# A two-layer hybrid diffusion backbone on one core: products further from their sums, Fourier sums on VectorE, GLA state as 18 tiles, softmax sums spread by one transfer

## The chip, the cores and the metric

The kernel runs as one program on one core of a Trainium2 chip. The metric is the device time of one execution in microseconds (us). The kernel before took 2532.82 us, the median of three runs (2531.42 to 2536.8). Five engines work side by side, each through its own queue of instructions in order: TensorE (PE in the profile), VectorE (DVE), ScalarE (ACT), GpSimd (POOL), and SyncE (SP), which here issues the DMA transfers.

## The reference

```python
for l in range(2):                      # 2048 latent tokens, 256 context tokens, width 1024
    shift, scale, gate = split(silu_c @ w_ada[l] + b_ada[l], 3)       # for x and for ctx
    hx = rmsnorm(x, norm_w[l]) * (1 + scale_x) + shift_x              # hc likewise
    (f, fg, nq, nk, nv, ng, gq, gk, gv, gg, zf, zb) = split(h @ w_in[l])
    four = (fft2(f by 4 groups of 64).real) @ w_four[l]               # over positions x channels
    na   = softmax(8 x 16 window scores + bias, context scores) @ v   # 6 heads of 64
    gla  = gated linear attention in both directions, 4 heads, dk 48, dv 96, then RMSNorm
    mix  = concat(four * silu(fg), na * silu(ng), gla * silu(gg))
    x    = x + gate_x * (mix @ w_out[l])                              # ctx too in layer 0
return rmsnorm(x, norm_f)
```

## The kernel before

Each layer goes through stages, one after another: the input projections it needs first, the Fourier group (`four`, from about 155 us in layer 0 and 1430 us in layer 1), the neighbourhood attention (`na`, from 210 and 1525 us), the gated linear attention (`gla`, from 793 and 2004 us) and the output projection (from 1150 and 2350 us). Tokens are worked in blocks of 512 (0 to 3 latent, 4 the context, 256 wide). Weights are loaded in float32, scaled and split into a high and a low half of 16 bits, so one product is three matmuls for each of eight slices of the width.

**Order.** Instructions recorded through the class `Pin` keep the order of the program on their engine; all of them show as L72 in the profile. The others (in `four`, and the gate products of L313) are put in order by the build, which may bring a product forward.

**Fourier.** `four` takes three levels, `f1` to `f3`, each on half the length of the one before: VectorE forms the differences `od` of the two halves of `u` (L387), POOL their sums in place (L388), VectorE two copies of two elements (L390, L391) and four sums and differences into `fo` (L392 to L395); TensorE multiplies `fo` by the transform (L374), and what remains of `u` last. `four_g` makes the gates of one block: two halves `j`, each 24 matmuls 512 wide (L313); `gates()` asks for block 0 in layer 0, blocks 0 to 3 in layer 1, after the third level.

**Attention.** A unit is a pair `p` of heads and a block `b`; there are 15 in layer 0 and 12 in layer 1. A planner (`fill`) puts the unit's steps, the next unit's preparations and the side jobs (`side`) into one order, spread by position; a transfer counts as a step with a gap of 6 planner us behind it. Side jobs bring the weights of later stages in (`w_steps`): load (`a_`), four reductions `red` of `ws` into `wsm` on VectorE and their `rest`, a product of a diagonal `dg` (by ACT) with ones on TensorE that turns the column of scales into rows (`mm`), its inverse, and eight conversions to 16 bits in turn on ACT and VectorE. Other side jobs make `ada_row`, the modulation of the next layer, eight chunks of it with a transposition on TensorE (`s2`), and the scales of the output projection (`wo_scale`).

**Sums of the softmax.** The `tail` of each unit has the sums of two heads as rows of 512 in partitions 0 and 64 (`rs`). `out_` writes them to DRAM (`rsd`, L761), `in_` reads them back spread over the partitions, 4 or 8 numbers each (`rc`, L765), `rec` takes the reciprocal on VectorE and writes to DRAM (`rrd`, L769), `bc_` reads that back to all partitions (L773), and `fin` has POOL multiply gate `gt` and result `ob`.

**Last unit and GLA.** During the last unit, `gla_pre` loads `gva` and `gvb` (the weights of GLA's values) through the one staging buffer `ws`, sets up constants (`s0`, `s2`: `wst`, `wab`, `zt`) and does the first token tile's products (`half`). The tail of the last unit is finished inside `gla`: `na_tail(0)` is reciprocal and write, `na_tail(1)` the multiplications. `gla` works on 18 tiles of 128 tokens in the order 16, 17, 0 to 15: `decay`, `vproj`, `qz`, `kk` are products of TensorE, `cums` the cumulated decays, from which POOL makes `QK` (scaled queries and keys); `upd` writes the states into `SU`, and `chain` accumulates along it. `nst.close()` gives the attention's tiles free; behind it `ATm` (two of 128 x 1024) and `SU` (one tile of 128 x 18 x 384) are set up, both cleared by POOL.

Of the kernel before, what the change touches and what calls it, by code (L numbers as in the profile page):

```python
# [9 lines left out]
F32 = mybir.dt.float32  # L10
# [5 lines left out]
ALU = mybir.AluOpType  # L16
# [4 lines left out]
P = 128  # L21
DM = 1024
KB = 8
# [3 lines left out]
NT = T // P  # L27
# [50 lines left out]
def body(ctx: ExitStack, tc: tile.TileContext, a, out, dbg=None):  # L78
# [52 lines left out]
    def ada(l, pool):  # L131
# [4 lines left out]
        def chunk(c, pool=pool):  # L136
            v, te = Pin(tc, V), Pin(tc, TE)
            d = {}

            @dma_step  # L140
            def s0():
                d["w"] = pool.tile([P, KB * 256], F32, tag="ws", name="ws", bufs=1).rearrange("p (k n) -> p k n", k=KB)
                nc.sync.dma_start(out=d["w"], in_=a["w_ada"][l, c])
                d["row"] = pool.tile([P, 256], F32, tag="row", name="ada_row", bufs=1)[0:2, :]
                nc.sync.dma_start(out=d["row"], in_=a["b_ada"][l:l + 1, c * 256:(c + 1) * 256].to_broadcast([2, 256]))

            def s1():
# [12 lines left out]
            def s2():  # L160
                pt = bank("b")
                for q in range(2):
                    te.transpose(out=pt[:, 2 * q:2 * q + 2], in_=d["row"][:, q * P:(q + 1) * P], identity=ident[0:2, 0:2])
                v.tensor_copy(sc[:, :, 2 * c:2 * c + 2], pt[:, 0:4].rearrange("p (q w) -> p w q", w=2))

            return [s0, s1, s1b] + ([s2] if c < 8 else [])

# [77 lines left out]

    def load_a(l, name, fin=True, pin=False):
        off, n = GOFF[name]
        st = wp.tile([P, KB * 256], F32, tag="ws", name="ws", bufs=1)[:, 0:KB * n]
        d = nc.sync.dma_start(out=st, in_=a["w_in"][l, :, KB * off:KB * (off + n)])
        if pin:  # L250
            tc.keep_in_program_order(d)
        w = (l, n, st, wp.tile([P, 8], F32, tag="wsm", name="wsm", bufs=8))
        return sum_c(*sum_b(*sum_a(w))) if fin else w
# [72 lines left out]

    def four_g(ug, b, W, te=TE, s=S, v=V):
        t0, n = BLOCKS[b]
        for j in range(2):
            pt = bank("pj")  # L330
            proj_ch(pt, W, j * P, t0, n, te=te)
            x1 = ug["pool"].tile([P, 512], F32, tag="x1", name="x1", bufs=2)
            silu(x1[:, 0:n], ug["g"][:, j, t0:t0 + n], pt[:, 0:n], W, v, s)
# [5 lines left out]
    def four(l, last, ug, gates, hooks):  # L339
# [7 lines left out]
        with ExitStack() as st:  # L347
# [35 lines left out]
            for nm in ("f1", "f2", "f3"):  # L383
# [3 lines left out]
                V.tensor_tensor(out=od[:, :, 0:h], in0=lo_, in1=hi_, op=ALU.subtract)  # L387
                G.tensor_tensor(out=u[:, :, 0:h], in0=lo_, in1=hi_, op=ALU.add)  # L388
                q2 = q // 2
# [49 lines left out]
            hook(99)  # L439
            gates()  # L440
            for b in ([] if last else [4]) + [0, 1, 2, 3]:
# [23 lines left out]

    def w_steps(l, name, put=None, pool=None, part=None, d=None, pin=False, sc=True, tag="b"):
        d = {} if d is None else d
        v, s, te = Pin(tc, V), Pin(tc, S), Pin(tc, TE)

        @dma_step  # L470
        def a_():
            d["w"] = load_a(l, name, fin=False, pin=pin)

# [39 lines left out]
        if part == 1:  # L513
            return conv
        return [a_] + [lambda i=i: red(i) for i in range(4)] + [rest, mm, inv] + ([] if part == 0 else conv)

    def na(l, last, W, side, st):
        with ExitStack() as bst:
# [236 lines left out]
            def tail(p, b, d):  # L755
                n = BLOCKS[b][1]
                m = 2 * n // P

                def out_():
                    for h in range(2):  # L760
                        nc.sync.dma_start(out=rsd[0:1, h * n:(h + 1) * n], in_=d["rs"][h * 64:h * 64 + 1, 0:n])  # L761

                def in_():
                    d["rc"] = wk.tile([P, 8], F32, tag="rc", name="rc")
                    nc.sync.dma_start(out=d["rc"][:, 0:m], in_=rsd[0:1, 0:2 * n].rearrange("a (p e) -> (a p) e", e=m))  # L765

# [13 lines left out]

                return [out_, in_, rec, bc_, fin]

# [204 lines left out]
            SA = 0.1  # L987
            rsd, rrd = (dr.tile([1, 1024], F32, name=f"{z}{l}") for z in ("rsd", "rrd"))
            for h in range(2):
# [50 lines left out]
            last_ = tail(*units[-1], ds[-1])  # L1040
            run(last_[0:2])

            def fin_tail(v, g, k):
                if k:
                    last_[4](g)
                else:
                    last_[2](v)
                    last_[3]()

            return fin_tail  # L1050

    def gla_pre(l, st, wk, c, nxt):
# [59 lines left out]
        for i, z in enumerate(more):  # L1112
            steps.insert(QP + 2 * i, z)
        return steps
# [12 lines left out]
    def gla(l, last, W1, W2, pre, p2done, na_tail, nst):  # L1127
        order2 = list(range((NL if last else NT) - 1, -1, -1))
        with ExitStack() as st:
            with ExitStack() as st1_:  # L1130
# [19 lines left out]
                def chain(eng, act, c, n, p0, sa, sb_):  # L1150
                    pr = slice(p0, p0 + DK)
                    if act:
                        eng.tensor_tensor(out=DF[pr, c, :], in0=TOT[pr, :, sa, c], in1=TOT[pr, :, sb_, n], op=ALU.add)
                        act.activation(out=DF[pr, c, :], in_=DF[pr, c, :], func=AF.Exp, scale=1.0 / 16.0)
                    sv = SU[pr, n, :]
                    eng.tensor_tensor(out=sv, in0=sv, in1=SU[pr, c, :], op=ALU.add)
                    sv4 = sv.rearrange("p (h v) -> p h v", h=NH)
# [108 lines left out]
                def upd(it):  # L1266
# [5 lines left out]
                    if t in fnext:  # L1272
                        v.tensor_copy(SU[0:DK, fnext[t], :], pu[0:DK, 0:384])
                    if t in bnext:
                        v.tensor_copy(SU[64:112, bnext[t], :], pu[64:112, 0:384])

# [41 lines left out]
                gnw = kp0.tile([P, DV], F32, name="gnw")  # L1318
                nc.sync.dma_start(out=gnw, in_=a["gnw"][l:l + 1, :].to_broadcast([P, DV]))
                DF = kp0.tile([P, NT, NH], F32, name="DF")  # L1320
                for i in range(2):
                    ATm.append(kpb.tile([P, 2, 512], F32, name=f"ATm{i}"))
                    g.memset(ATm[i], 0.0)
                for t in (16, 17, 15, 0):
                    g.memset(SU[:, t, :], 0.0)
                for it in range(NT):
                    nx = it + 1 < NT
                    if 2 <= it < 16:
                        g.memset(SU[:, it - 1, :], 0.0)
                    if it > 0:  # L1330
# [9 lines left out]
                    if nx:  # L1340
                        kk(it + 1)
                        zT_(it + 1)
# [18 lines left out]
            with ExitStack() as st2_:  # L1361
# [44 lines left out]
                def inter(s_):  # L1406
                    s_["po"] = po = bank("a")
                    for h in range(NH):
                        te.matmul(out=po[:, h * DV:(h + 1) * DV], lhsT=s_["qt"][:, h * P:(h + 1) * P], rhs=SU[:, s_["t"], h * DV:(h + 1) * DV], start=True, stop=True)

# [66 lines left out]
    def wo_scale(l, c):  # L1477
# [24 lines left out]

        return [s0, s1] + ([lambda: None, s1b, s2] if c == 3 else [])

# [243 lines left out]
    for l in range(2):  # L1748
# [5 lines left out]

        def gates():
            for b in (0, 1, 2, 3) if last else (0,):
                four_g(ug[0], b, Wg)
# [21 lines left out]
        def side(p, b, wk):  # L1779
            n = p + 1  # L1780
            res = []
            if b == 0:
                res += w_steps(l, f"kv{n}", store(W, ("kv", n))) if n < 3 else w_steps(l, "gqz", store(nxt, "gqz"))
            if b == 2:
                res += w_steps(l, f"qg{n}", store(W, ("qg", n))) if n < 3 else w_steps(l, "gk", store(nxt, "gk"))
            if (p, b) == (2, 3):
# [199 lines left out]
```

## Time and profile before

| | |
|---|---|
| median of three runs | 2532.82 us (2531.42 to 2536.8) |
| the profiled execution | 2537.43 us, its span 2535.6 |
| TensorE busy | 2333.9 us, 92% |
| VectorE, ACT, POOL busy | 1609.2 (63%), 1126.5 (44%), 1117.4 (44%) |

The span is what the trace shows of the execution, from its first to its last instruction; the execution's own time is 1.8 us longer. TensorE runs at one of two clocks, and "granted clock" is the mean of a stretch as a share of the faster one. In a timeline, what stands in brackets is how long the engine had been idle before the instruction, and whose work ended that. "SPq" is a transfer being issued by SyncE.

### The profile page before, as it was taken

Reading aid. Unit: us, or ns where it says so; the run is one execution under the profiler, and the core shown is the slowest. Engines: PE = TensorE matmul, PEld = TensorE weight load, DVE = VectorE, ACT = ScalarE, POOL = GpSimd, SP = SyncE. Lnnn points to the kernel's source line nnn. Section 1 sums busy time; section 2 is a strip of 40 time slices with the busy share of each in tenths; the row PEclk is TensorE's granted clock in tenths of the full one; section 3 lists DMA queues with packets and bytes.
Section 4 is the critical chain, followed back from the end, with each engine's and each line's share of the span. In section 5 each row is a group of like instructions: output and inputs, shape, how many; then the busy total and the mean of one; then the engine's idle time right before and its main releaser. Section 6 shows DMA issues by size and latency. Waiting matters only on the chain. (4 is left out here: it accounts for less than half of the span.)

```text
span 2535.6 us, 44432 instructions
## 1 busy us (share of the span) xinstructions
PE 2333.9 (92%) x16878; PEld 1554.5 (61%) x16878; DVE 1609.2 (63%) x3607; ACT 1126.5 (44%) x2049; POOL 1117.4 (44%) x1303
## 2 busy tenths in 40 slices
PE   5989998999978999999889999999999699999998
PEld 3555454454546999895444554555555589989444
DVE  5765666666865666695665435667666566669554
ACT  3523554555555444342333224666656434444222
POOL 1534444455544444453334234555555444445232
PEclk7999999999989999999999999999999899999999
DMA  6304124124222100364433021141221210126442
GB/s 250 117 3 131 60 83 123 49 86 121 88 62 66 44 34 35 102 191 154 138 121 110 31 67 49 54 105 55 62 64 34 72 36 35 38 80 200 154 150 100
DMA packets 128298, 225.16 MB, mean 89 GB/s; under 512 B 18346, under 2 KB 81444, under 8 KB 122452
## 3 DMA queue, kind: packets, MB, share of 16 engines
q1 hardware_dynamic: 122900, 212.68, 24.9%
q0 software_dynamic: 5184, 9.64, 2.6%
q8 instruction: 133, 2.18, 0.4%
q14 instruction: 81, 0.66, 0.1%
HBM read 176.89 MB, written 51.47 MB: 90 GB/s over the span
## 5 line engine op out<-in xcount | busy, mean ns | idle before, releaser
L72 PE MATMUL b_pj<-hx,w 128*128 128x512 f16 (+1 forms) x3168 | 690.7, 365 | 0.9 <-DVE w L72 0.9
L72 POOL TENSOR_TENSOR pl<-pt,ph 128x512 f16<-128x512 f32 (+6 forms) x300 | 307.5, 1026 | 433.8 <-ACT ph L72 365.7
L72 PEld LDWEIGHTS <-w 128*128 128x128 f16 x3168 | 305.8, 99 | 276.6 <-issue 15.0
L72 PEld LDWEIGHTS <-hx 128*128 128x128 f16 x5088 | 440.5, 100 | 11.0 <-issue 4.7
L72 PE MATMUL b_pj<-w,hx 128*128 128x192 f16 (+2 forms) x4272 | 396.9, 252 | 4.5 <-DVE zt L72 4.5
L72 PE MATMUL b_pj<-wo,m 128*128 128x512 f16 x816 | 306.2, 384 | 0.0
L72 PE MATMUL b_a<-wo,m 128*128 128x512 f16 x816 | 305.7, 384 | 0.0
L72 PEld LDWEIGHTS <-m 128*128 128x128 f16 x1632 | 161.8, 99 | 190.4 <-issue 9.0
L72 DVE SCALAR_TENSOR_TENSOR pt<-b_a,sc,TS 128x160 f32<-128x160 f32 (+4 forms) x432 | 153.1, 400 | 154.4 <-PE b_a L72 113.6
L72 ACT ACTIVATE pt<-pt,psh 128x480 f32<-128x480 f32 (+1 forms) x192 | 121.7, 634 | 168.2 <-DVE pt L72 158.1
L72 PE MATMUL b_c<-ph,vt 128*128 128x320 f16 (+5 forms) x888 | 179.2, 295 | 0.9 <-ACT ph L72 0.9
L72 PEld LDWEIGHTS <-vt 128*128 128x128 f16 x1332 | 120.8, 100 | 86.2 <-issue 23.2
L72 ACT CAST ph<-pt 128x512 f16<-128x512 f32 (+6 forms) x300 | 166.5, 555 | 9.5
L72 POOL TENSOR_TENSOR xn<-xn,xt 128x512 f32<-128x512 f32 x66 | 82.4, 1270 | 178.0 <-DVE xn L72 178.0
L72 PE MATMUL b_a<-Q,K 128*128 128x320 f16 (+5 forms) x444 | 120.9, 295 | 10.4 <-ACT Q L72 10.2
L72 PE MATMUL b_c<-pl,vt 128*128 128x320 f16 (+5 forms) x444 | 126.9, 295 | 3.6 <-POOL pl L72 3.6
L72 PE MATMUL b_a<-q,k 128*128 128x320 f16 (+5 forms) x444 | 121.6, 295 | 3.5 <-DVE MX L72 1.8
L72 DVE CUSTOM_DVE_ANT_0 b_b<-b_b,tmi 128x512 f32<-128x512 f32 (+3 forms) x144 | 86.5, 601 | 60.0 <-PE b_b L72 58.8
L72 ACT ACTIVATE pt<-b_a,psh,sc 128x512 f32<-128x512 f32 (+1 forms) x108 | 81.0, 750 | 67.1 <-PE b_a L72 61.8
L72 POOL TENSOR_TENSOR hx<-hu,hx 128x512 f16<-128x512 f32 x54 | 69.5, 1302 | 72.6 <-DVE hx L72 72.2
L72 POOL TENSOR_TENSOR ats<-ATm 128x512 f32<-128x512 f32 x34 | 43.3, 1274 | 129.0 <-DVE ATm L72 129.0
L72 PEld LDWEIGHTS <-q 128*128 128x128 f16 x540 | 51.5, 98 | 79.1 <-issue 24.1
(271 smaller groups left out, 4262.7 us busy)
## 6 DMA issues: line engine op xcount, KB each, us to landing
mx<-mixd SPq DMA_DIRECT2D x34, 512.0 KB
ws<-in_w_in SPq DMA_DIRECT2D x16, 1024.0 KB
xt<-in_x SPq DMA_DIRECT2D x32, 512.0 KB
ws<-in_w_ada SPq DMA_DIRECT2D x16, 1024.0 KB
ws<-in_w_out SPq DMA_DIRECT2D x16, 1024.0 KB
TS<-in_ts SPq DMA_DIRECT2D x12, 1000.0 KB
xres<-xn SPq DMA_DIRECT2D x18, 512.0 KB
qdt_d<-qkT SPq DMA_DIRECT2D x34, 256.0 KB
```

Source lines behind the costliest of these rows:

```text
L72: return self.tc.keep_in_program_order(f(*args, **kw))
```

## The change

1. `ada`: one empty step between a chunk's addition on VectorE and its transpositions on TensorE, for the eight chunks of layer 0's attention.
2. `w_steps` gets `lag`: for `kv`, `qg`, `gqz`, `gk` one more step lies between the last reduction and the product (`rest` stands twice in the list; its second call has nothing left to do). `wo_scale` gets one more empty step.
3. Fourier: the sums of the halves are made by VectorE, behind `fo`; the gates of block 0 are split into halves `j`: half 0 is asked for in the first level, ahead of its transforms, half 1 (and blocks 1 to 3 of layer 1) where the gates were.
4. `gla_pre`: a second staging tile `ws2` for `gvb`, in space that `rope` takes later; both loads come first, the steps of the two weights are interleaved by a list written by hand, and the products stand three or four steps behind the reductions.
5. `tail`: `rsd` goes; two transfers spread `rs` straight from one partition to 64. `na_tail(0)` comes behind `decay(0)` and `vproj(0, 1)`, `na_tail(1)` behind `cums(0)` and `vproj(1, 0)`.
6. `gla`: `kk(1)` comes ahead of `nst.close()`. `SU` is 18 tiles, laid out in the order 17, 15, 0, 16, 1 to 14; VectorE clears `ATm` and the first four of them, POOL the others as before.

```diff
-            return [s0, s1, s1b] + ([s2] if c < 8 else [])
+            return [s0, s1, s1b] + ([lambda: None, s2] if c < 8 else [])
...
-        st = wp.tile([P, KB * 256], F32, tag="ws", name="ws", bufs=1)[:, 0:KB * n]
+        st = stage(KB * n) if stage else wp.tile([P, KB * 256], F32, tag="ws", name="ws", bufs=1)[:, 0:KB * n]
...
-    def four_g(ug, b, W, te=TE, s=S, v=V):
+    def four_g(ug, b, W, te=TE, s=S, v=V, js=(0, 1)):
         t0, n = BLOCKS[b]
-        for j in range(2):
+        for j in js:
...
                 V.tensor_tensor(out=od[:, :, 0:h], in0=lo_, in1=hi_, op=ALU.subtract)
-                G.tensor_tensor(out=u[:, :, 0:h], in0=lo_, in1=hi_, op=ALU.add)
...
+                V.tensor_tensor(out=u[:, :, 0:h], in0=lo_, in1=hi_, op=ALU.add)
                 ntl = q // P
+                if nm == "f1":
+                    gates(0)
...
-            gates()
+            gates(1)
...
-        return [a_] + [lambda i=i: red(i) for i in range(4)] + [rest, mm, inv] + ([] if part == 0 else conv)
+        return [a_] + [lambda i=i: red(i) for i in range(4)] + [rest] * lag + [mm, inv] + ([] if part == 0 else conv)
...
-                def out_():
-                    for h in range(2):
-                        nc.sync.dma_start(out=rsd[0:1, h * n:(h + 1) * n], in_=d["rs"][h * 64:h * 64 + 1, 0:n])
-
                 def in_():
                     d["rc"] = wk.tile([P, 8], F32, tag="rc", name="rc")
-                    nc.sync.dma_start(out=d["rc"][:, 0:m], in_=rsd[0:1, 0:2 * n].rearrange("a (p e) -> (a p) e", e=m))
+                    for h in range(2):
+                        nc.sync.dma_start(out=d["rc"][h * 64:h * 64 + 64, 0:m], in_=d["rs"][h * 64:h * 64 + 1, 0:n])
...
-                return [out_, in_, rec, bc_, fin]
+                return [in_, rec, bc_, fin]
...
-        steps = [s00]
-        for i, n in enumerate(("gva", "gvb")):
-            steps += w_steps(l, n, c["W"].append, pool=lambda: c["kp"])
-            if i == 0:
-                steps[1:1] = [s0]
-        steps.insert(9, s2)
+        def s01():
+            c["tmp"] = tst = ExitStack()
+            c["st"] = tst.enter_context(sb("gkt"))
+
+        va = w_steps(l, "gva", c["W"].append, pool=lambda: c["kp"])
+        vb = w_steps(l, "gvb", c["W"].append, pool=lambda: c["kp"], stage=lambda n: c["st"].tile([P, n], F32, name="ws2"))
+        vb[0] = (lambda f: lambda: f())(vb[0])
+        steps = [s00, s01, s0, vb[0], va[0]] + va[1:5] + vb[1:3] + [s2, va[6], vb[3], va[7], vb[4]] + va[8:12] + [vb[6], va[12], vb[7]] + va[13:] + vb[8:]
...
-            steps.insert(QP + 2 * i, z)
+            steps.insert(QP - 2 + 2 * i, z)
...
                 vproj(0, 0)
-                na_tail(v, g, 0)
                 decay(0)
                 vproj(0, 1)
+                na_tail(v, g, 0)
                 qz(1)
-                na_tail(v, g, 1)
                 cums(0)
                 vproj(1, 0)
+                na_tail(v, g, 1)
+                kk(1)
                 nst.close()
...
-                SU = kp0.tile([P, NT, 384], F32, name="SU")
+                SU = {t: kp0.tile([P, 384], F32, name=f"SU{t}") for t in [17, 15, 0, 16] + list(range(1, 15))}
...
-                    g.memset(ATm[i], 0.0)
-                for t in (16, 17, 15, 0):
-                    g.memset(SU[:, t, :], 0.0)
+                    v.memset(ATm[i], 0.0)
+                for t in (17, 15, 0, 16):
+                    v.memset(SU[t], 0.0)
...
-        return [s0, s1] + ([lambda: None, s1b, s2] if c == 3 else [])
+        return [s0, s1] + ([lambda: None, lambda: None, s1b, s2] if c == 3 else [])
...
-                res += w_steps(l, f"kv{n}", store(W, ("kv", n))) if n < 3 else w_steps(l, "gqz", store(nxt, "gqz"))
+                res += w_steps(l, f"kv{n}", store(W, ("kv", n)), lag=2) if n < 3 else w_steps(l, "gqz", store(nxt, "gqz"), lag=2)
```

## Rows read from the trace of the kernel before

**Rows 1.** the page: busy time, share of the span and instructions of each engine

```profile
PE 2333.9 (92%) x16878; PEld 1554.5 (61%) x16878; DVE 1609.2 (63%) x3607; ACT 1126.5 (44%) x2049; POOL 1117.4 (44%) x1303
```

**Rows 2.** waits of TensorE: waiter, releaser, us in all, times, longest

```profile
PE b_b L72 <- ACT dg L72: 31.6, 14, 4.1
...
PE b_a L374 <- DVE fo L393: 8.6, 2, 4.3
```

**Rows 3.** windows: width, busy PE, PEld, DVE, ACT, POOL; clock, DMA share, GB/s

```profile
1975.00:2000.00 25.00, 15.05 (x116) 9.26 (x114) 17.43 (x49) 15.24 (x28) 12.41 (x13) 0.93 0.28 91
...
2000.00:2025.00 25.00, 18.04 (x138) 16.14 (x139) 6.59 (x22) 7.83 (x14) 9.05 (x13) 0.70 0.17 56
```

**Rows 4.** timeline of Fourier level 1, layer 0: start, duration, engine, instruction, [idle before]

```profile
154.48 2.29 DVE L387 TENSOR_TENSOR od<-u 128x2048 f32<-128x2048 f32 x1 [9.09 <-ACT u L72]
...
155.73 2.11 PE L313 MATMUL b_pj<-hx,w 128*128 128x512 f16 x9
...
156.81 0.17 DVE L390 COPY fo<-od 128x2 f32<-128x2 f32 x1
...
156.86 4.50 POOL L388 TENSOR_TENSOR u<-u 128x2048 f32<-128x2048 f32 x1 [19.43 <-DVE od L387]
...
156.89 4.49 DVE L391 COPY fo<-od 128x2 f32<-128x2 f32 x1
...
162.12 2.05 PE L374 MATMUL b_a<-Mx,fo 128*128 128x256 f32 x4 [4.28 <-DVE fo L393]
...
164.38 3.19 PE L374 MATMUL b_a<-Mx,fo 128*128 128x256 f32 x8
...
190.17 1.03 PE L374 MATMUL b_a<-Mx,u 128*128 128x256 f32 x4
```

**Rows 5.** timeline of TensorE, attention of layer 0: two later products

```profile
440.05 0.37 PE L72 MATMUL b_b<-ident,ada_row 2*128 2x2 f32 x2 [1.81 <-DVE ada_row L72]
...
734.45 0.79 PE L72 MATMUL b_b<-dg,ones 128*128 128x128 f32 x2 [3.60 <-ACT dg L72]
```

**Rows 6.** timeline of TensorE, last attention unit of both layers

```profile
789.40 0.49 PE L72 MATMUL b_b<-dg,ones 128*128 128x128 f32 x2 [3.07 <-ACT dg L72]
...
1981.19 0.49 PE L72 MATMUL b_b<-dg,ones 128*128 128x128 f32 x2 [2.85 <-ACT dg L72]
...
1988.46 1.15 PE L72 MATMUL b_pj<-w,hx 128*128 128x192 f16 x12 [3.85 <-DVE zt L72]
...
2000.64 0.80 PE L72 MATMUL b_b<-dg,ones 128*128 128x128 f32 x2 [3.50 <-ACT dg L72]
```

**Rows 7.** timeline, start of GLA in both layers, and a clear by VectorE

```profile
764.46 0.38 DVE L72 MEMSET wst<- 128x384 f32 x1
...
808.08 0.66 PE L72 MATMUL b_b<-ident,QK 128*128 128x128 f32 x4 [2.13 <-POOL QK L72]
...
2011.77 0.20 DVE L72 RECIPROCAL rc<-rc 128x8 f32<-128x8 f32 x1 [6.10 <-DMA rc<-rsd]
...
2012.88 0.36 PE L72 MATMUL b_a<-lr,tri 128*128 128x192 f32 x1 [2.57 <-DVE lr L72]
...
2021.64 2.02 PE L72 MATMUL b_c<-v,QK 128*128 128x96 f32 x8 [3.52 <-POOL QK L72]
...
2024.75 0.55 DVE L72 COPY SU<-b_c 48x384 f32<-48x384 f32 x1 [8.83 <-POOL SU L72]
```

**Rows 8.** timeline of the sums of two tails, both in layer 1

```profile
1939.66 0.24 SPq L761 DMA_DIRECT2D rsd<-rs  x1
...
1940.85 0.34 SPq L765 DMA_DIRECT2D rc<-rsd  x1
...
1945.47 0.19 DVE L72 RECIPROCAL rc<-rc 128x8 f32<-128x8 f32 x1
...
2005.63 0.25 SPq L761 DMA_DIRECT2D rsd<-rs  x1
...
2009.35 0.33 SPq L765 DMA_DIRECT2D rc<-rsd  x1
```

More of the change, by code (lines that the diff above doesn't have):

```diff
@@ L244, in put_e, with load_a @@
                 hook(g)
-    def load_a(l, name, fin=True, pin=False):
+    def load_a(l, name, fin=True, pin=False, stage=None):
         off, n = GOFF[name]
-        st = wp.tile([P, KB * 256], F32, tag="ws", name="ws", bufs=1)[:, 0:KB * n]
+        st = stage(KB * n) if stage else wp.tile([P, KB * 256], F32, tag="ws", name="ws", bufs=1)[:, 0:KB * n]
         d = nc.sync.dma_start(out=st, in_=a["w_in"][l, :, KB * off:KB * (off + n)])
@@ L464, in spread, with w_steps @@
         return out_ + b_[j:]
-    def w_steps(l, name, put=None, pool=None, part=None, d=None, pin=False, sc=True, tag="b"):
+    def w_steps(l, name, put=None, pool=None, part=None, d=None, pin=False, sc=True, tag="b", lag=1, stage=None):
         d = {} if d is None else d
@@ L471, in a_ @@
         def a_():
-            d["w"] = load_a(l, name, fin=False, pin=pin)
+            d["w"] = load_a(l, name, fin=False, pin=pin, stage=stage)
         def red(i):
@@ L987, in na @@
             SA = 0.1
-            rsd, rrd = (dr.tile([1, 1024], F32, name=f"{z}{l}") for z in ("rsd", "rrd"))
+            rrd = dr.tile([1, 1024], F32, name=f"rrd{l}")
             for h in range(2):
@@ L1040, in na @@
             last_ = tail(*units[-1], ds[-1])
-            run(last_[0:2])
+            run(last_[0:1])
             def fin_tail(v, g, k):
                 if k:
-                    last_[4](g)
+                    last_[3](g)
                 else:
-                    last_[2](v)
-                    last_[3]()
+                    last_[1](v)
+                    last_[2]()
             return fin_tail
@@ L1128, in gla @@
         order2 = list(range((NL if last else NT) - 1, -1, -1))
+        pre["tmp"].close()
         with ExitStack() as st:
@@ L1154, in chain @@
                         act.activation(out=DF[pr, c, :], in_=DF[pr, c, :], func=AF.Exp, scale=1.0 / 16.0)
-                    sv = SU[pr, n, :]
-                    eng.tensor_tensor(out=sv, in0=sv, in1=SU[pr, c, :], op=ALU.add)
+                    sv = SU[n][pr, :]
+                    eng.tensor_tensor(out=sv, in0=sv, in1=SU[c][pr, :], op=ALU.add)
                     sv4 = sv.rearrange("p (h v) -> p h v", h=NH)
@@ L1272, in upd @@
                     if t in fnext:
-                        v.tensor_copy(SU[0:DK, fnext[t], :], pu[0:DK, 0:384])
+                        v.tensor_copy(SU[fnext[t]][0:DK, :], pu[0:DK, 0:384])
                     if t in bnext:
-                        v.tensor_copy(SU[64:112, bnext[t], :], pu[64:112, 0:384])
+                        v.tensor_copy(SU[bnext[t]][64:112, :], pu[64:112, 0:384])
                 def intra(it):
@@ L1328, in gla @@
                     if 2 <= it < 16:
-                        g.memset(SU[:, it - 1, :], 0.0)
+                        g.memset(SU[it - 1], 0.0)
                     if it > 0:
@@ L1340, in gla @@
                     if nx:
-                        kk(it + 1)
+                        if it > 0:
+                            kk(it + 1)
                         zT_(it + 1)
@@ L1408, in inter @@
                     for h in range(NH):
-                        te.matmul(out=po[:, h * DV:(h + 1) * DV], lhsT=s_["qt"][:, h * P:(h + 1) * P], rhs=SU[:, s_["t"], h * DV:(h + 1) * DV], start=True, stop=True)
+                        te.matmul(out=po[:, h * DV:(h + 1) * DV], lhsT=s_["qt"][:, h * P:(h + 1) * P], rhs=SU[s_["t"]][:, h * DV:(h + 1) * DV], start=True, stop=True)
                 def store(s_):
@@ L1753, in body, with gates @@
                 four_x(ug[0], b, Wx)
-        def gates():
-            for b in (0, 1, 2, 3) if last else (0,):
+        def gates(k):
+            four_g(ug[0], 0, Wg, js=(k,))
+            for b in (1, 2, 3) if last and k else ():
                 four_g(ug[0], b, Wg)
@@ L1782, in side @@
             if b == 0:
-                res += w_steps(l, f"kv{n}", store(W, ("kv", n))) if n < 3 else w_steps(l, "gqz", store(nxt, "gqz"))
+                res += w_steps(l, f"kv{n}", store(W, ("kv", n)), lag=2) if n < 3 else w_steps(l, "gqz", store(nxt, "gqz"), lag=2)
             if b == 2:
-                res += w_steps(l, f"qg{n}", store(W, ("qg", n))) if n < 3 else w_steps(l, "gk", store(nxt, "gk"))
+                res += w_steps(l, f"qg{n}", store(W, ("qg", n)), lag=2) if n < 3 else w_steps(l, "gk", store(nxt, "gk"), lag=2)
             if (p, b) == (2, 3):
```

## The prediction

> **What bounds the kernel now.** First the page's busy line: TensorE is busy for 2333.9 us of the span [rows 1], far more than any other engine, so a microsecond counts where TensorE stands idle or runs at the lower clock, and work that other engines lose or gain counts only through it. Second, the waits of TensorE by what ended them [rows 2]: the 31.6 us behind ACT's `dg` (14 times) and the 8.6 us behind `fo` (twice) are waits of steps that this change moves. Third, two 25-us windows around the end of the last attention unit of layer 1 [rows 3]: in the first TensorE is busy for 15.05 us, in the second for 18.04 us at a mean granted clock of 0.70 of full speed. An idle gap there is paid twice, since the clock falls to the 1.2 GHz level after it and the products behind it run longer. Last, the timeline at each place that the diff touches [rows 4 to 8].
>
> **Fourier sums and gate products.** `od` ends at 156.77 (154.48 + 2.29). POOL then adds the two halves of `u` for 4.50 us, and VectorE's copy of two elements takes 4.49 us, the same stretch to 0.03 us; its neighbour of the same size, L390, takes 0.17. TensorE has ten gate products to run in that time and then waits 4.28 us for `fo`; its next twelve products take 2.05 + 3.19 = 5.24 us, where four of the same shape at full clock take 1.03, so 3.1 for twelve: 2.1 us lost to the clock [rows 4]. The second wait of the 8.6 us is layer 1's [rows 2], so this holds twice. With the add off POOL, `fo`'s first piece is there near 157.9 (156.98, where L390 ends, one more copy like it and one subtraction, which I put at 0.7 us since it works on a quarter of `od`'s elements), and with all 24 products of one gate half ahead (nine took 2.11, so 24 take 5.6) TensorE is busy until about 160: both the gap and the slow products go, 4.28 + 2.1 = 6.4 per layer, 12.8 in all. Against it: 14 products that go ahead no longer fill later holes, 14 x 0.23 = 3.3 us in layer 0, where one block has a gate; layer 1 has four blocks and loses less, say 1. The add itself is placed behind all four `fo` operations; VectorE pays about 2.3, 1.2 and 0.6 us for it (the first by `od`'s duration, the others by its half and quarter), while TensorE transforms. I take 12.8 - 4.3 = 8.5, call it **9**; bounds 4 (holes reopen at the sums) and 13.
>
> Here a rule of the Trainium skill bears: "SBUF — State Buffer", section "Who interferes with whom", has VectorE and GpSimd (POOL) share a pair of ports under an exclusive lock; the loser stands still for the whole instruction. This trace agrees with 4.49 beside 4.50. The same section has an operation of VectorE with two SBUF inputs contend with a reading operation of POOL, which speaks against moving the add; by that rule the term would fall towards its lower bound of 4 if POOL had work at each of the adds, and stay 9 if it has none.
>
> **Later products in attention (`lag=2`, the `ada` and `wo_scale` empty steps).** Each moves TensorE's step one planner step away from the VectorE or ACT step that feeds it. Layer 0's attention has four waits for `ada_row` of 1.0 to 2.0 us, 6.8 in all, of which one stands in [rows 5]; `wo_scale` has one of 3.60 [rows 5]. The empty step adds the TensorE work of one planner step; I estimate that it covers most of a wait of 2 us and only part of one of 3.60. I take 4 of the first and 1 of the second: **5**. Bounds 0 (VectorE reaches its step as much later) and 10 (all of it).
>
> **The last unit of each layer (`gla_pre`).** The products that give the scales of `gva` and `gvb` wait some 3 us each in layer 0 (the second is shown), 2.85 and 3.50 in layer 1, where the first half of the `gk` product also waits 3.85 for `zt`, which VectorE makes behind four conversions of weights [rows 6]. With two staging tiles the second load needn't wait for the first's conversions, both sets of reductions come early, and each product has three or four steps behind its last reduction instead of two. Idle: 6.0 and 10.2. VectorE is at 17.43 of 25 there [rows 3] and does not more than before. I take 5 of 6.0 + 1 for the clock, less 1 for a new wait: **5**; and 8 of 10.2 in layer 1: **8**. Bounds 3 and 17 together: `gva` is now issued behind `gvb`, and a VectorE reduction that waits for its load holds everything queued behind it, the attention's own `pt` operations first.
>
> **The sums of the last tail, and the start of GLA.** In layer 1 VectorE waits 6.10 us at the reciprocal, and the operations queued behind it, which make `lr`, keep TensorE waiting for 2.57; behind the tail's two multiplications POOL makes `QK`, for which TensorE waits 3.52, and then clears `ATm` and `SU`, for which VectorE's copy waits 8.83 [rows 7]. The change takes one hop out: 1.19 us from issue to issue where nothing is in the way (1939.66 to 1940.85), 3.72 us here (2005.63 to 2009.35), behind the load of `gga` [rows 8]; it puts reciprocal and multiplications behind `decay(0)`, `vproj` and `cums(0)`, so that `QK` comes ahead of them on POOL, and it gives TensorE `kk(1)` to do. The clears cost VectorE 0.38 us for 128 x 384 (the row of the same size) [rows 7], four times, and about 1.0 twice for `ATm` (1024 against 384 elements): 3.6 us, which lie on VectorE's path, since they wait for the tail's tiles to come free and VectorE works in order; POOL's clears kept VectorE 8.83 us. Removed: the 2.57 and the 3.52. Of the second window's loss to the clock (18.04 x 0.30 = 5.4 us at most) this and the last unit's gaps share, and I count 2 here. 2.57 + 3.52 + 2 less 2 for the clears: **6**. In layer 0 the wait for `QK` is 2.13 [rows 7] and I count 1 for the rest: **3**. Bounds for both: 0 and 17. `SU` as 18 tiles costs nothing by itself: it changes only what a copy must wait for.
>
> Most of the other 25 reciprocals find their sum there: at 1945.47 one follows its neighbour with no wait, 4.6 us after the second transfer's issue [rows 8]. There the hop removed is hidden, and I count 0.
>
> **Sum.** 9 + 5 + 5 + 8 + 6 + 3 = 36 us. The profiled execution took 2537.4 (span 2535.6), so 2501.4; the median of the runs shown, 2532.8, is 4.6 under that execution, so **2497**.
>
> **Rivals.** (1) *The stalls move.* The attention stages leave TensorE few holes, and the lag only shows the next one: VectorE, with its adds, its clears and reductions that wait for loads, becomes what the products wait for. Then the Fourier gap goes (9) and some 6 of the remaining 27: 15, giving 2518. For it: VectorE at 17.43 of 25 in the last unit with PE at 15.05 [rows 3], so neither is full and the order decides. Against: the waits named are for single steps, with other work queued behind them.
> (2) *Slower: the spread transfer lands late.* The sum's row now goes straight from one partition to 64, 32 bytes each, and the reciprocal stands earlier in VectorE's order: I estimate some 2.4 us behind the row's first transfer, half of the 5.8 it has now (1939.66 to 1945.47). A hop takes 1.19 by [rows 8], and 3.72 behind a load. Each microsecond of landing over 2.4 holds VectorE in up to 27 units, where attention is waiting for `pt`; at 1.3 us too late (3.7 us) the 36 us are eaten, at 4.5 us 27 x 2.1 = 57 us go, giving 2497 + 57 = 2554. Against it: the transfer out of DRAM that it replaces wrote the same 32-byte pieces and was on time. "DMA: Bandwidth & Descriptors", section "Specifications" of the Trainium skill, has transfers under 512 bytes fall to read-modify-write, which would speak for this rival; the on-time reciprocals of [rows 8] show no such price.
> (3) *It doesn't do what it says.* The build already brings gate products forward and VectorE's clears still wait for the tail: 5 us or fewer, 2528 to 2533.
>
> **How the numbers follow.** Forecast (2483 to 2512) 0.68, rival 1 0.17, rival 2 0.08, rival 3 0.07. About 0.2%, 5 us, is what a measurement of this kernel can tell from no change: faster is the forecast, rival 1 and a little of rival 3 (0.86), same the rest of rival 3 (0.06), slower rival 2 (0.08). The lower end is the upper bounds of the parts, 13 + 10 + 17 + 17 = 57, taken together: 2476. The upper end takes in rival 1 with some room, 2522, and leaves out rivals 2 and 3 and the rim of rival 1, 0.2 in all.
>
> **What would show it.** Fourier: the copy of L391 at 0.2 us, the wait before L374 gone, its first products near 0.26 each. Attention: waits behind `dg` from 31.6 to under 20 us. Last unit: TensorE over 18 us in the window that had 15.05. GLA's start: no wait of VectorE at the reciprocal, `SU`'s copy waiting under 2 us, the clock over 0.85. Wrong it would be if VectorE shows new waits behind `rc` or `ws`, or if holes open at the second Fourier sums.

## The result and the profile after

The changed kernel takes 2507.8 us (median of four runs, 2499.06 to 2508.53), the kernel before 2534.7 beside it: a ratio of 0.9885, 95% interval 0.987 to 0.9899, or 26 to 33 us less, 27 by the medians. The forecast was 36 less, 2497. Sign and range hold; a quarter of the gain is missing. The profiled execution took 2508.12 us, its span is 2506.4, 29.2 less than before's.

Of the changed kernel: the page's busy line, four waits of TensorE (what for, us in all, times, longest) and three windows (width; busy PE, PEld, DVE, ACT, POOL; clock, DMA share, GB/s).

```profile
PE 2325.9 (93%) x16878; PEld 1550.3 (62%) x16878; DVE 1612.0 (64%) x3625; ACT 1123.8 (45%) x2049; POOL 1091.7 (44%) x1285
...
PE b_b L72 <- ACT dg L72: 19.9, 11, 4.1
PE b_a L72 <- ACT Q L72: 12.7, 14, 2.1
...
PE b_c L72 <- POOL pl L72: 9.3, 14, 2.5
PE b_b L72 <- POOL q L72: 9.0, 9, 2.6
...
150.00:175.00 25.00, 25.00 (x116) 16.88 (x114) 19.77 (x35) 6.99 (x15) 0.40 (x1) 1.00 0.00 1
...
1957.00:1982.00 25.00, 17.79 (x130) 10.53 (x129) 18.36 (x54) 15.57 (x29) 11.41 (x11) 0.93 0.17 54
1987.00:2012.00 25.00, 21.45 (x240) 20.09 (x238) 12.45 (x29) 8.63 (x20) 8.23 (x12) 1.00 0.17 56
```

Against [rows 1 to 3]: the waits behind `dg` fell by 11.7 us, and those behind `fo` are off the list. But TensorE now waits 9.3 us for POOL's `pl` and 9.0 for its `q`, where the kernel before had less:

```profile
PE b_b L72 <- POOL q L72: 3.9, 7, 1.1
...
PE b_c L72 <- POOL pl L72: 3.6, 8, 0.9
```

The last unit's window (1975 to 2000 before, 1957 to 1982 now) rose from 15.05 to 17.79 us of TensorE, and GLA's start runs at full clock.

To see where the time went, the trace of every kernel is cut at the same events, and each number below is the difference of two times in a timeline, in us. **F**: first `od` of a layer to its first score product. **A**: on to the end of the softmax sums of the last unit but one. **U**: on to GLA's first `decay` product. **D**: first to second `decay` product. **G0**: on to layer 1's first `od`. **R**: to the end. 0 and 1 are the layers; the kernels below "changed" are the experiments.

```
                       F0    A0    U0    D0    G0     F1    A1    U1    D1     R
before               94.8 514.5  30.4  20.2 616.8  118.2 424.6  33.3  20.7 507.5
changed              89.6 508.8  29.7  14.0 615.9  111.2 433.7  30.4  11.5 507.5
Fourier alone        89.4 515.2  30.5  20.5 616.5  111.2 425.4  31.7  21.7 507.6
sums on POOL         95.9 510.4  27.8  13.9 615.8  117.5 433.0  29.6  11.5 505.9
gates late           88.6 507.8  27.0  13.9 612.4  111.4 433.6  30.3  11.5 507.8
late tail            89.4 513.4  27.6  13.9 615.8  111.2 426.6  29.2  11.5 505.8
late multiplications 89.4 509.4  30.1  13.9 612.5  111.4 426.8  28.8  11.5 505.4
spread alone         95.2 509.7  30.8  16.1 616.2  118.4 429.5  34.8  17.8 507.6
no lag               89.4 510.3  27.9  13.9 614.5  111.4 429.7  30.6  11.5 507.3
old last unit        89.4 507.0  31.9  13.9 614.0  111.4 433.4  34.3  11.5 508.7
GLA's start alone    94.8 515.8  32.1  13.9 614.2  117.4 424.8  33.3  11.5 506.8
clears on POOL       89.4 508.7  28.1  18.0 615.0  111.3 435.5  30.3  15.5 508.0
both repairs         89.4 509.0  30.5  13.9 612.6  111.4 422.6  29.2  11.5 505.7
both, last unit late 89.6 508.7  30.3  13.9 615.0  111.2 424.1  30.5  11.5 507.1
```

Where two kernels have the same code, F and D repeat within 1 us (within 0.2 in the changed code), A within 2 to 3.5, U0 and G0 only within 3 to 4.5. G0 goes with the granted clock: it is 612.4 to 612.6 where the mean of the stretch was 0.983, and 615.8 to 616.8 where it was 0.975. So a stretch tells more than a whole time: a median of a few us more or less may be all U0 and G0.

The first two lines are the account of the 29.2 us: Fourier 5.2 + 7.0, layer 0's attention 5.7, the last units 0.7 + 2.9, the starts of GLA 6.2 + 9.2, 1.4 elsewhere, and **layer 1's attention minus 9.1**, where nothing was forecast.

### The profile page after: what moved, and what is told of

It reads as the page before. It is cut to its first block, busy times and chain, and to the rows that moved or that the text cites. A ratio compares the mean times of both kernels' runs of the same rounds, so it can differ in the third digit from the quotient of the medians.

```text
span 2506.4 us, 44391 instructions
## 1 busy us (share of the span) xinstructions
PE 2325.9 (93%) x16878; PEld 1550.3 (62%) x16878; DVE 1612.0 (64%) x3625; ACT 1123.8 (45%) x2049; POOL 1091.7 (44%) x1285
```

## The experiments

**Fourier: the whole part alone, and without each half.** Three kernels. The first puts the Fourier part into the kernel before. The other two undo one half of it in the changed kernel:

```diff
 # sums on POOL
+                G.tensor_tensor(out=u[:, :, 0:h], in0=lo_, in1=hi_, op=ALU.add)
...
-                V.tensor_tensor(out=u[:, :, 0:h], in0=lo_, in1=hi_, op=ALU.add)
```

```diff
 # gates late
-                if nm == "f1":
-                    gates(0)
...
+            gates(0)
             gates(1)
```

The Fourier part alone:

> The kernel before with the Fourier part alone: sums on VectorE, gate products of half a block ahead of the first transforms. In the changed kernel the stretch from the first od to the first score product was 5.2 us shorter in layer 0 and 7.0 in layer 1. If these belong to the Fourier part, this kernel is 12 us faster than before (10 to 14). If part of it is the clock that varies from run to run, 4 to 9.

2524.48 us, ratio 0.9955 (0.9939 to 0.9972), 10.6 less; F is 5.4 and 7.0 shorter, as in the changed kernel.

Sums on POOL:

> The changed kernel with the sums of the Fourier halves back on POOL; the gate products stay ahead of the first transforms. The copy of two elements beside POOL's sum should take 4.5 us again. If the gate products alone cover the wait (24 instead of 10 of them, 3.1 us more), the kernel is 0 to 4 us slower than the changed one. If VectorE's freedom is what counts in all three levels, 5 to 9 slower.

2515.23 us, ratio 0.992 (0.9903 to 0.9936). F is 6.3 us longer than in the changed kernel in both layers, hardly different from before. The timeline of level 1 and 2, layer 0, in this kernel:

```profile
156.03 4.50 POOL L388 TENSOR_TENSOR u<-u 128x2048 f32<-128x2048 f32 x1 [19.43 <-DVE od L387]
...
156.06 4.50 DVE L391 COPY fo<-od 128x2 f32<-128x2 f32 x1
...
161.29 3.17 PE L374 MATMUL b_a<-Mx,fo 128*128 128x256 f32 x12 [1.26 <-DVE fo L393]
...
164.36 2.34 POOL L388 TENSOR_TENSOR u<-u 128x1024 f32<-128x1024 f32 x1 [3.83 <-DVE od L387]
164.38 2.35 DVE L390 COPY fo<-od 128x2 f32<-128x2 f32 x1
...
170.42 2.07 PE L374 MATMUL b_a<-Mx,fo 128*128 128x256 f32 x4 [3.71 <-DVE wsm L72]
```

Two copies of two elements again last as long as POOL's sum beside them. With 24 gate products ahead the first wait is 1.26 instead of the 4.28 of [rows 4], but a later one of 3.71 opens, with half of the filler spent.

Gates late:

> The changed kernel with all gate products asked for after the third level again; the sums stay on VectorE. With the sums on POOL and the gates ahead the Fourier stretches were 5.5 and 6.2 us longer than in the changed kernel. If the VectorE add alone carries the gain, this kernel is within 2 us of the changed one. If both are needed, since fo comes near 157.9 and ten gate products end at 157.8 but nothing covers the later levels, it is 4 to 10 us slower.

2501.03 us, ratio 0.9874 (0.9858 to 0.9891); F is 88.6 and 111.4, no longer than in the changed kernel. So the sums on VectorE carry the Fourier gain alone, and asking for gate products early adds nothing to it. The median is 6.8 us under the changed kernel's, which neither expectation had; between the profiled executions most of the difference lies in U0 and G0 (2.7 and 3.5), and whether the gates have part in it stays open. In the changed kernel the stretch looks like this:

```profile
156.40 0.16 DVE L390 COPY fo<-od 128x2 f32<-128x2 f32 x1
...
158.88 2.29 DVE L396 TENSOR_TENSOR u<-u 128x2048 f32<-128x2048 f32 x1
...
160.21 2.92 PE L374 MATMUL b_a<-Mx,fo 128*128 128x256 f32 x12
```

**Attention: one step more in the tail, in two places.** The theory: with one step fewer in the tail, the rest of it comes one planner step earlier, and POOL's multiplications now stand ahead of `q`.

```diff
 # late tail
-                return [in_, rec, bc_, fin]
+                return [in_, lambda: None, rec, bc_, fin]
 # late multiplications
-                return [in_, rec, bc_, fin]
+                return [in_, rec, bc_, lambda: None, fin]
```

> The changed kernel with one more empty step in the tail, between the spreading transfer and the reciprocal, so that reciprocal, broadcast and POOL's two multiplications stand where the kernel before had them; the transfer through DRAM stays removed. Between the first score product of layer 1 and the end of the sums of its last but one unit the changed kernel took 433.7 us where before took 424.6. Theory A (the tail comes too early: POOL multiplies gt and ob ahead of q, VectorE waits at the reciprocal): TensorE's wait for POOL q falls from 6.7 back to 1.4 us in that stretch, the stretch to about 425 to 428, and the kernel is 5 to 9 us faster than the changed one, near 2500. Theory B (the loss comes from the later products of w_steps or from the clock alone): POOL q may come earlier, but the stretch stays at 431 to 434 and the time within 2 us of the changed kernel.

2499.9 us, ratio 0.9861 (0.9846 to 0.9875), 7.9 under the changed kernel: A1 is 426.6, and the wait for `q` in it is back at 1.4 us. A0, however, is 4.6 longer than in the changed kernel.

> The changed kernel with one more empty step in the tail, between the broadcast and POOL's multiplications: the reciprocal stays early, only the multiplications go back to their old place. If POOL's queue is what the early tail costs, this gives the same as the empty step ahead of the reciprocal, 5 to 9 us under the changed kernel. If VectorE's waits at the early reciprocal cost it (it waited 2.1 us in the units with the 2.6 us wait for q), less than half of that comes back, 0 to 3 us. Under theory B nothing does.

2497.1 us, ratio 0.9848 (0.983 to 0.9867), 10.7 under the changed kernel by the medians (between the profiled executions 3.4 us lie in G0). A1 is as short, 426.8, with 1.7 us of waits for `q` instead of 6.7, and A0 stays at 509.4. So it is POOL's queue, not VectorE's early reciprocal, that costs layer 1's attention 7 us; the early reciprocal is what gains layer 0's 4 to 5, through which wait no run shows. Layer 1, third unit of the first pair, in the changed kernel and then in the one with late multiplications:

```profile
1606.11 0.20 DVE L72 RECIPROCAL rc<-rc 128x8 f32<-128x8 f32 x1 [2.09 <-DMA rc<-rs]
...
1612.55 1.31 POOL L72 TENSOR_TENSOR gt<-gt,rs 128x512 f32<-128x512 f32 x1
1613.93 1.27 POOL L72 TENSOR_TENSOR ob<-ob,gt 128x512 f32<-128x512 f32 x1
1615.28 2.37 POOL L72 TENSOR_TENSOR q<-qf,q 64x512 f16<-64x512 f32 x2
...
1616.49 0.31 PE L72 MATMUL b_b<-k,q 128*128 128x320 f16 x1 [2.61 <-POOL q L72]
```

```profile
1610.21 2.38 POOL L72 TENSOR_TENSOR q<-qf,q 64x512 f16<-64x512 f32 x2
...
1611.41 0.31 PE L72 MATMUL b_b<-k,q 128*128 128x320 f16 x1
...
1613.96 1.31 POOL L72 TENSOR_TENSOR gt<-gt,rs 128x512 f32<-128x512 f32 x1
```

What matters is the order: `gt` and `ob`, 2.6 us together, run ahead of `q` in the first and behind it in the second. TensorE waits 2.61 us for `q` in the first and not at all in the second.

**The spread alone, in the kernel before.**

> The kernel before with the softmax sums spread by one transfer alone; reciprocal, broadcast and multiplications come one planner step earlier, nothing else is changed. Theory A (the early multiplications stand ahead of q and pl on POOL): layer 1's attention, from the first score product to the sums of the last but one unit, grows from 424.6 us to 430 to 434, and the kernel is slower than before by 3 to 9 us, 2538 to 2544, although a transfer has gone. Theory B (the loss in the changed kernel needs the later products too): within 2 us of before, or faster by 1 to 4 for the shorter chain at the end of each layer.

2532.98 us, ratio 0.9993 (0.9984 to 1.0002): no change. The time is what theory B said, but not for its reason, for the stretches nearly show theory A's loss (429.5, where 430 was its lower end) with gains beside it: A1 is 4.9 longer and U1 1.5 longer, but A0 4.8 shorter and the two D 7.0 shorter together. What I had left out in theory A was the gain in layer 0 and that at GLA's start. The loss in A1 comes without the later products, which is against theory B.

**No lag.** The changed kernel without the empty steps of `ada`, `wo_scale` and `w_steps`:

```diff
-            return [s0, s1, s1b] + ([lambda: None, s2] if c < 8 else [])
+            return [s0, s1, s1b] + ([s2] if c < 8 else [])
...
-                res += w_steps(l, f"kv{n}", store(W, ("kv", n)), lag=2) if n < 3 else w_steps(l, "gqz", store(nxt, "gqz"), lag=2)
+                res += w_steps(l, f"kv{n}", store(W, ("kv", n))) if n < 3 else w_steps(l, "gqz", store(nxt, "gqz"))
```

> The changed kernel without the empty steps in ada, wo_scale and w_steps (lag of 1 everywhere). Layer 0's attention from the first score product to the sums of the last but one unit took 514.5 us before and 508.8 in the changed kernel. If the later products gained this, 5 us were the forecast, this kernel is 4 to 7 us slower than the changed one. If they gain little (TensorE's waits for ada_row fell only from 6.8 to 5.3 us there), it is 0 to 3 slower, and the 5.7 us come from the tail that is one step shorter, whose early multiplications do no harm in layer 0.

2501.33 us, ratio 0.9869 (0.9854 to 0.9883), whose interval overlaps the changed kernel's; by the median it is 6.5 faster, where both expectations had it slower or the same. A0 is 1.5 longer, within what A scatters, and A1 is **4.0 shorter**: the later products gain next to nothing in layer 0 and cost 4 in layer 1. The queue of ACT there, in the changed kernel and in the one called "both repairs", which has the old lag:

```profile
1560.84 0.72 ACT L72 ACTIVATE w<-ws,wsm 128x512 f16<-128x512 f32 x1
1561.58 0.58 ACT L72 CAST Q<-b_b 64x512 f16<-64x512 f32 x1
...
1562.21 0.38 PE L72 MATMUL b_a<-Q,K 128*128 128x512 f16 x1 [2.06 <-ACT Q L72]
```

```profile
1558.86 0.58 ACT L72 CAST Q<-b_b 64x512 f16<-64x512 f32 x1
...
1559.49 0.38 PE L72 MATMUL b_a<-Q,K 128*128 128x512 f16 x1 [1.43 <-ACT Q L72]
```

One step of lag shifts every later step of the list too, and here a conversion of weights (0.72 us) lands in front of `Q`, for which TensorE waits 2.06 us in the changed kernel and 1.43 in the other. The waits for `Q` over all of A1 fall from 10.2 to 7.5 us; in the kernel with late multiplications, which has the lag, they are 10.4.

**The last unit.** The changed kernel with `gla_pre` as before:

> The changed kernel with the last unit's preparations (one staging buffer, old order of gla_pre) as before. From the sums of the last but one unit to those of the last the changed kernel takes 27.7 us in layer 0 and 29.0 in layer 1, before took 30.3 and 31.6. If the reordering gained just that, this is 5 us slower than the changed kernel (4 to 7). If it gained what was forecast, 13, and something else took it back there, it is 10 to 13 slower. If the shorter stretch comes from the tail and not from the reordering, within 2 us of the changed kernel.

2510.86 us, ratio 0.991 (0.9896 to 0.9925), 3 us over the changed kernel. From sums to sums the last unit takes 31.6 and 32.8 us here, against 27.7 and 29.0 in the changed kernel. The reordering itself is thus worth 4 per layer, less than the 13 forecast for both. The median shows less than half of it, but A0 and G0, whose code is the same, happen to be 1.8 and 1.9 shorter in this profiled execution. Nor is all of it a gain on the kernel before, whose last units take 30.3 and 31.6: with the old order the changed kernel is over 1 us slower there, and so, in layer 1, is the kernel before with the early tail alone (33.1). The waits of TensorE in layer 1's last unit, here and then in the changed kernel:

```profile
PE b_b L72 <- ACT dg L72: 6.0, 2, 3.5
PE b_pj L72 <- DVE zt L72: 4.3, 1, 4.3
```

```profile
PE b_c L72 <- POOL pl L72: 5.0, 6, 2.5
PE b_c L72 <- ACT ph L72: 1.3, 2, 0.8
PE b_a L72 <- DVE pt L72: 0.7, 1, 0.7
PE b_b L72 <- ACT dg L72: 0.7, 1, 0.7
```

The waits named in the prediction go, 10.3 to 0.7, and others of 7.0 come, on the attention's own chain `pt`, `ph`, `pl`. The first suspect was POOL's multiplications, at 1966.02 to 1968.8, in front of the `pl` that comes 2.49 us late. They were put two steps later in this unit (three empty steps ahead of `fin` for the tail that runs in it, one elsewhere), in the kernel with both repairs:

> The kernel with both repairs, and in the last unit of each layer the multiplications of the tail before it two steps later still. In the kernel with late multiplications they run from 1956.5 to 1959.2 there; two casts of VectorE, 0.35 us elsewhere, take 1.32 each beside them, zt is late by 2.1 us and POOL's pl behind them. If these collisions hold the last unit, its stretch in layer 1 (27.6 us) shortens by 1.5 to 3 us and layer 0's likewise: 2 to 5 us under the kernel with both repairs. If TensorE's waits there come from ACT, whose conversions of gvb stand between the softmax's own operations, it is the same within 1.5 us.

2494.69 us, ratio 0.9843 (0.9828 to 0.9857), 3.5 over the kernel with both repairs, which neither expectation had; the last unit's stretch in layer 1 is 28.9 us against 28.0 there and 29.0 in the changed kernel. So one step later may have taken 1 us out, two steps more nothing, and the suspicion falls for the rest. With both repairs TensorE waits in this unit 2.4 us for `pl`, 1.1 for `ph` and 2.1 for `zt`; with the two steps more it is 3.1, 2.1 and 1.9. What remains is ACT's own queue, in the changed kernel:

```profile
1979.38 0.60 ACT L72 ACTIVATE w<-ws,wsm 128x384 f16<-128x384 f32 x1
1979.89 0.68 ACT L72 ACTIVATE pt<-pt,psh 128x480 f32<-128x480 f32 x1
1980.60 0.59 ACT L72 CAST ph<-pt 128x480 f16<-128x480 f32 x1
...
1981.25 0.30 PE L72 MATMUL b_c<-ph,vt 128*128 128x160 f16 x2 [0.79 <-ACT ph L72]
```

Conversions of weights stand between the softmax's operations, without a gap on ACT, at the unit's end. By the order of the steps these are `gva`'s four, from 1976.46 on, 10 us behind the product of its scales; in the kernel before they ran from 1983.45 to 1986.9, in the middle of the unit and 2 us behind their product. `gvb`'s four come last in both (from 1982.49, and from 2002.18 before). That this order holds the softmax is read, not tested: no kernel was run that takes the conversions away.

**GLA's start.** Alone in the kernel before, and the changed kernel with the clears back:

```diff
 # clears on POOL
-                    v.memset(ATm[i], 0.0)
+                    g.memset(ATm[i], 0.0)
...
-                    v.memset(SU[t], 0.0)
+                    g.memset(SU[t], 0.0)
```

> The kernel before with the start of GLA alone: reciprocal and multiplications of the last tail behind decay, vproj and cums, kk(1) ahead, SU as 18 tiles, the first clears on VectorE; the transfer through DRAM stays. In the changed kernel the stretch from the first to the second decay product was 6.2 us shorter in layer 0 and 9.2 in layer 1. If that comes from the order, this kernel gains 12 to 16 us on before. If it comes from the transfer that is removed (3.7 us between the two issues in layer 1, 3.6 in layer 0), it gains 7 to 9.

2518.68 us, ratio 0.9937 (0.9922 to 0.9952), 16.4 less; D is 13.9 and 11.5, all of what the changed kernel has. Here the transfer that the change removes adds nothing.

> The changed kernel with the clears of ATm and of the first four SU tiles back on POOL. From the first to the second decay product the changed kernel takes 14.0 us in layer 0 and 11.5 in layer 1, before took 20.2 and 20.7. POOL's clears took 3.3 us in a row. If the clears on VectorE carry part of the gain, this is 2 to 6 us slower than the changed kernel in these two stretches together. If the order (QK ahead of the tail's multiplications, kk(1) early) carries it alone, within 1.5 us.

2516.79 us, ratio 0.9931 (0.9917 to 0.9946): D is 18.0 and 15.5, 4.0 longer in each layer, more than the 2 to 6 expected for both together. Without the clears on VectorE more than half of D's gain of 15.4 is lost. In this kernel, layer 1:

```profile
2002.04 1.84 POOL L72 MEMSET ATm<- 128x1024 f32 x2
2003.82 1.50 POOL L72 MEMSET SU<- 128x384 f32 x4
...
2004.27 1.14 DVE L72 COPY SU<-b_c 48x384 f32<-48x384 f32 x2 [8.34 <-POOL SU L72]
2005.44 0.29 DVE L72 CAST zT<-b_a 128x128 fp32r<-128x128 f32 x1
...
2005.88 0.66 PE L72 MATMUL b_a<-wab,zT 128*128 128x384 f32 x1 [5.72 <-DVE zT L72]
```

and in the changed kernel:

```profile
1993.74 0.91 DVE L72 MEMSET ATm<- 128x1024 f32 x1 [0.92 <-POOL QK L72]
1994.82 0.91 DVE L72 MEMSET ATm<- 128x1024 f32 x1 [0.16 <-issue]
1995.76 1.60 DVE L72 MEMSET SU<- 128x384 f32 x4
1997.28 1.08 DVE L72 COPY SU<-b_c 48x384 f32<-48x384 f32 x2
...
1996.05 1.27 POOL L72 TENSOR_TENSOR gt<-gt,rs 128x512 f32<-128x512 f32 x1 [2.58 <-DMA rs<-rrd]
...
1998.82 0.41 PE L72 MATMUL b_a<-wab,zT 128*128 128x384 f32 x1 [1.76 <-DVE zT L72]
```

`zT`, which the second `decay` needs, stands behind the copy into `SU` on VectorE, and the copy waits for the clears, which on POOL are queued behind the tail's multiplications. VectorE clears before these have even run: its clears begin at 1993.74, the multiplications at 1996.05.

In the kernel before, the same wait of VectorE at the copy, 8.83 us in [rows 7], cost TensorE nothing:

```profile
2023.46 3.99 PE L72 MATMUL b_pj<-w,hx 128*128 128x192 f16 x24
...
2027.60 0.29 DVE L72 CAST zT<-b_a 128x128 fp32r<-128x128 f32 x1 [1.71 <-PE b_a L72]
```

TensorE was running 24 products meanwhile (`kk(1)`), and VectorE, done with the copy, waited another 1.71 us for TensorE. The change brings `kk(1)` ahead, so that nothing covers the copy's wait any more: with the clears on POOL, TensorE stands for 5.72 us. The order and the clears gain what they gain together.

**Both repairs together**: late multiplications, and a lag of 1 in `w_steps` (the empty steps of `ada` and `wo_scale` stay).

> The changed kernel with both repairs: POOL's multiplications of the tail one step later, and the products of w_steps back at a lag of 1 (the empty steps of ada and wo_scale stay). Alone they gave 10.7 and, with all lags undone, 6.5 us. If the lag costs by itself (TensorE waits 8.2 us for Q in layer 1's attention with it, 6.4 without; 3.2 us by stretches), this is 2 to 6 us under the kernel with late multiplications, 2491 to 2495. If the two losses were one and the same (POOL too early against q), it is within 1.5 us of it, 2496 to 2498.

2491.18 us, ratio 0.983 (0.9816 to 0.9845), 16.6 under the changed kernel by the medians and clear of it by the intervals; between the profiled executions A1 has 11.1 of 16.0 us, and most of the rest lies in G0 (3.3) and R (1.8), whose code is the same. A1 is 422.6: the multiplications (433.7 to 426.8) and the lag (426.8 to 422.6) are two causes that add up, and layer 1's attention is now 2 us shorter than before.

All fourteen kernels of the table fall into line with that. A1 is 433.0 to 435.5 in the five with early multiplications and the lag, 429.5 and 429.7 with early multiplications alone, 426.6 and 426.8 with the lag alone, and 422.6 to 425.4 in the five with neither. A0 is 513.4 to 515.8 in the four with the late reciprocal and 507.0 to 510.4 in the ten with the early one.

## Why the prediction was right, and where not

**Fourier, 9 forecast, 12.2 found.** The cause, POOL's sum holding VectorE's two-element copy, is as argued, and the trace of the kernel with the sums on POOL agrees twice more with the rule of the Trainium skill named there ("SBUF — State Buffer", "Who interferes with whom"): 4.50 beside 4.50 and 2.35 beside 2.34. The rule's warning against the move does not bite: POOL has 0.40 us of work in the window, and VectorE's sum takes 2.29 (L396), like `od`. The deduction of 4.3 for filler that is lost was wrong: F is shorter by nearly all of the 12.8. The credit to the gate products was wrong too: without them ahead, F is the same.

**Later products, 5 forecast, 5.7 found in A0, but not from them.** The number is right and the step is not. That is luck. Without the lag A0 is 510.3 instead of 508.8, with the reciprocal late 513.4: layer 0 gains from the reciprocal's place, which I had counted at 0. The four waits for `ada_row` fell only from 6.8 to 5.3 us, and the wait of `wo_scale`, 3.60 in [rows 5], is still 3.6 us long. And I costed the lag at nothing outside the products: it shifts the conversions behind it, and one of them met `Q` on ACT, 4 us in A1.

**The tail in the other units, 0 forecast, minus 7 found in layer 1.** This step failed, and with the lag's 2 to 4 it is the loss of 9.1. The prediction followed the sum to VectorE's reciprocal and stopped; it did not follow what is moved with it, the two multiplications on POOL, and did not ask who is queued behind them there. Rival 1 named the class (a new wait replaces the old) and gave VectorE as its place; it was POOL, and next ACT.

**Rival 2 fell.** The earliest reciprocal behind a spread in the changed kernel starts 1.71 us after the row's end, where I put the limit at 2.4. The 32-byte pieces, for which the Trainium skill ("DMA: Bandwidth & Descriptors", "Specifications") has read-modify-write, come in time here; no run has larger pieces to compare. Some rows do land later than the limit: at 1960.70 VectorE has waited 1.98 us for one that was complete at 1956.90, and it waits 2.1 us in the unit shown above. No harm to TensorE shows in that: A1 is 426.6 with the reciprocal late and 426.8 with it early.

**The last units, 5 + 8 forecast, 0.7 + 2.9 found in U** (2.6 + 2.6 from sums to sums). The named waits went as forecast, 10.3 to 0.7 in layer 1. The term was mis-sized: it kept back 2.2 of the 10.2 us in layer 1, and new waits of 7.0 came. The stretch had been taken as idle time with nothing behind it; neither ACT nor VectorE was full ([rows 3]), but the attention's chain runs through both. What holds that chain is open in part, as said above.

**GLA's start, 6 + 3 forecast, 9.2 + 6.2 found.** The order was right; the clears on VectorE were counted as a cost of 2 and are a gain of 8 for both layers. The sum left out the 8.83 us that VectorE waited for `SU` in [rows 7], and rightly so for the kernel before, where TensorE's products covered them; it did not ask what would cover them once `kk(1)` had gone ahead. The clears did not wait for the tail's multiplications either.

Sum of what was found: 12.2 + 5.7 + 3.6 + 15.4 less 9.1, and 1.4 elsewhere, 29.2 on the profiled executions. Errors of both signs make the forecast look better than its steps: two terms are 10 too small together, one is 9 too large, and one was missing.

## What to carry to other kernels

When a step is taken out of a list, follow everything that comes earlier with it, on each engine's queue, and ask which operation of the critical chain it now stands in front of: two multiplications of 2.6 us, harmless where they were, cost 7 us, a quarter of what this change gained. Move the step that was slow, and put an empty step where the others would slide. A wait of an engine that is not the bottleneck costs nothing only as long as the bottleneck has other work for that time: 8.8 us of VectorE at a copy were free before, and with that work moved ahead they would have cost 4 us in each layer.

## What the runs showed of the hardware

VectorE's copies and casts were stretched by POOL's work beside them more often than the one place that was forecast. In layer 1's last unit of the changed kernel two casts of 32 x 384 take 1.31 and 1.33 us beside POOL's multiplications. The same two took 0.35 and 0.36 in the kernel before, where POOL stood idle beside them (last line):

```profile
1966.02 1.48 POOL L72 TENSOR_TENSOR gt<-gt,rs 128x512 f32<-128x512 f32 x1 [1.69 <-DMA rs<-rrd]
...
1966.40 1.31 DVE L72 CAST wab<-wlo 32x384 fp32r<-32x384 f32 x1
1967.72 1.33 DVE L72 CAST wlo<-wlo 32x384 fp32r<-32x384 f32 x1
...
1981.99 0.35 DVE L72 CAST wab<-wlo 32x384 fp32r<-32x384 f32 x1
```

A transfer from one partition to 64, 32 bytes each, was read by VectorE 1.71 us after its source was written, at the earliest. And clears of the same size cost the two engines about the same: for 128 x 1024, 0.91 us on VectorE (1.08 from the start of one to that of the next) and 0.92 on POOL (1.84 for two).
